# Rotating an 8192x8192 matrix: the last macro tile's outputs divided by rows in place of its loads by columns, and another rotation of the buffers at the end

## The chip, the cores and the metric

The kernel runs on one core of one Trainium2 chip. The metric is the device time of one execution in microseconds (us); lower is better. Before the change, three runs took 1270.16, 1271.46 and 1272.62 us: a median of 1271.46.

## The reference

```python
def setup_inputs():
    return {"x": np.random.randn(8192, 8192).astype(np.float32), "k": 1}

def reference(x: np.ndarray, k: int) -> np.ndarray:
    return np.rot90(x, k)
```

With k = 1 this is a turn by 90 degrees counterclockwise: out[i, j] = x[j, 8191 - i]. The kernel reads 256 MiB from HBM and writes 256 MiB; nothing is calculated.

## The kernel before

A turn is a transpose with one axis reversed. The input is cut into 16 macro tiles of 1024 rows by 4096 columns (`R` by `W`), numbered 0 to 15 (`LAST` is 15); tile m covers half the width of one band of 1024 rows. In this text (m,i) is step i of macro tile m: load (15,6) is the seventh load of the last tile, store (14,7) the last store of the one before.

**Three stages.** A load (`load`, issued by SP) brings 2 MB into a load buffer of `a_pool`: for all tiles but the last, 128 rows by 4096 columns, so that each of the 128 partitions takes one contiguous row piece of 16 KB (line 107). A reversal (`reverse`, line 111, on VectorE) copies the load buffer into `grid` with the 128 columns of each block in reversed order. `grid` holds one whole macro tile (128 KB in each partition), as 8 row blocks by 8 column chunks of 512 columns. A store (`store`) makes 2 MB of output: 32 transposes of 128x128 on TensorE (line 130) into two PSUM tiles of 128x2048, one copy of each PSUM tile into an output buffer by ScalarE (line 147), and one DMA to HBM issued by ScalarE (line 149).

**The grid is used twice over.** Even tiles store row block t in `grid[:, t]`, odd ones in `grid[:, :, t]`. Store (m,i) reads column chunk i of all eight row blocks, which is just the part of `grid` that row block i of the next tile takes. So the main loop runs, for each m under 15 and each i: issue load (m+1,i), make store (m,i), reverse load (m+1,i) into the part that the store has freed. Reversals of tile 0 come before it, the eight stores of tile 15 after it.

**A store's shape.** Store (m,i) for m under 15 covers 512 columns of the input, so 512 rows of the output, and 1024 columns of the output (the tile's 1024 input rows): a DMA of 4 x 128 pieces of 1024 numbers, 4 KB each. Output buffers are read as whole 16 KB rows by the DMA (`whole_reads` rewrites the source's access pattern so).

**The last tile.** If its stores needed all eight row blocks, as the others do, none could start before its last load. So its loads are divided by columns (lines 96 to 104): load (15,t) takes 256 rows by 2048 columns, as two pieces of 8 KB in each partition; loads 0 to 3 make the left half of the columns, 4 to 7 the right half. Stores (15,0) to (15,3) need the left half alone, (15,4) to (15,7) the right half. `chunk` translates the place in the grid (lines 83 to 84).

**Buffers.** `a_pool` and `o_pool` have two buffers of 16 KB in a partition each, taken in turn. A new load needs the load buffer of two loads before, reversed. A new store needs the output buffer of two stores before, landed in HBM. At the end, when no loads are left to be issued, stores take load buffers too (line 118): store (14,7), and stores (15,1), (15,3), (15,5), (15,7). As load (15,7) is taken ahead of store (14,7), that store gets the buffer of load (15,6), and store (15,1) that of load (15,7).

**Order.** Each engine works through its instructions in program order. SP issues loads only; ScalarE carries out the copies and issues the stores, so that a copy that waits holds up the copies and DMA issues of all later stores. Loads and stores go through one DMA queue each (q1 and q10 in the profile), on the same 16 DMA engines.

Of the kernel before, what the change touches and what calls it, by code (L numbers as in the profile page):

```python
# [2 lines left out]

# [5 lines left out]

P = 128  # L10
T = 8
R = T * P
W = 4096
C = W // T
F = 4096
FP = 2048


def whole_reads(nc):

    for fn in nc.m.functions:
        for block in fn.blocks:
            for n, ins in enumerate(block.instructions):
                if not isinstance(ins, mybir.InstDMACopy):
                    continue
                src = ins.ins[0]
                ap = [list(d) for d in src.ap]
                if len(ap) == 3 and ap[2][0] == 1 and ap[1][0] == ap[2][1]:
                    ap = [ap[0], [1, 1], [1, ap[1][1] * ap[2][1]]]
                    block.instructions[n] = copy.replace(  # L30
                        ins,
                        ins=[copy.replace(src, ap=ap)],
                        ant_dge_precooked=False,
                    )


@with_exitstack
def kernel(
    ctx: ExitStack,
    tc: tile.TileContext,  # L40
    x: bass.AP,
    k: bass.AP,
    out: bass.AP,
):

    nc = tc.nc
    assert k == 1, f"only k=1 supported, got {k}"
    nc.at_finalize(whole_reads)

    N, M = x.shape
    dt = x.dtype

    consts = ctx.enter_context(tc.tile_pool(name="consts", bufs=1))  # L60
    ident = consts.tile([P, P], dt)
    make_identity(nc, ident)
    grid = consts.tile([P, T, T, C], dt)

    a_pool = ctx.enter_context(tc.tile_pool(name="a_pool", bufs=2))
    o_pool = ctx.enter_context(tc.tile_pool(name="o_pool", bufs=2))
    psum_pool = ctx.enter_context(
        tc.tile_pool(name="psum", bufs=2, space=bass.MemoryType.PSUM)
    )

    tiles = [(r0, c0) for r0 in range(0, N, R) for c0 in range(0, M, W)]
    LAST = len(tiles) - 1
    G = F // R
    PW = FP // R
    H = T // 2

    def row_tile(m, t):

        return grid[:, t] if m % 2 == 0 else grid[:, :, t]

    def chunk(m, t, i):

        if m == LAST:
            q, t = t % 2 * H + i % H, i // H * H + t // 2
        else:
            q = i
        return grid[:, t, q] if m % 2 == 0 else grid[:, q, t]

    def load(m, t):

        r0, c0 = tiles[m]
        if m == 0 and t % 4 >= 2:
            a = o_pool.tile([P, W], dt, tag="o")
        else:
            a = a_pool.tile([P, W], dt, tag="a")
        if m == LAST:
            r0 += t % H * 2 * P
            c0 += t // H * (W // 2)
            nc.sync.dma_start(
                out=a[:].rearrange("r (t c) -> r t c", t=2),  # L100
                in_=x[r0 : r0 + 2 * P, c0 : c0 + W // 2].rearrange(
                    "(t r) c -> r t c", t=2
                ),
            )
        else:
            r0 += t * P
            nc.sync.dma_start(out=a[:], in_=x[r0 : r0 + P, c0 : c0 + W])  # L107
        return a

    def reverse(m, t, a):  # L110
        nc.vector.tensor_copy(  # L111
            out=row_tile(m, t).rearrange("r c (b m) -> r c b m", m=P),
            in_=a[:].rearrange("r (c b m) -> r c b m", c=T, m=P)[:, :, :, ::-1],
        )

    def store(m, i):
        r0, c0 = tiles[m]
        if m == LAST - 1 and i == T - 1 or m == LAST and i % 2:
            ot = a_pool.tile([P, F], dt, tag="a")
        else:  # L120
            ot = o_pool.tile([P, F], dt, tag="o")
        o = ot[:].rearrange("m (g f) -> m g f", g=G)
        ps = []
        for h in range(G // PW):
            pt = psum_pool.tile([P, FP], mybir.dt.float32, tag="ps")
            ps.append(pt[:].rearrange("m (g f) -> m g f", g=PW))

        def transposes(h, w, t):
            b = h * PW + w
            nc.tensor.transpose(  # L130
                ps[h][:, PW - 1 - w, t * P : (t + 1) * P],
                chunk(m, t, i)[:, b * P : (b + 1) * P],
                ident,
            )

        by_row = i == 0 and m < LAST
        if by_row:
            for t in range(T):
                for h in range(G // PW):
                    for w in range(PW):  # L140
                        transposes(h, w, t)
        for h in range(G // PW):
            if not by_row:
                for w in range(PW):
                    for t in range(T):
                        transposes(h, w, t)
            nc.scalar.copy(o[:, G - PW - h * PW : G - h * PW, :], ps[h])  # L147
        top = M - c0 - (i + 1) * G * P
        nc.scalar.dma_start(  # L149
            out=out[top : top + G * P, r0 : r0 + R].rearrange(  # L150
                "(g m) f -> m g f", g=G
            ),
            in_=o,
        )

    for t in range(T):
        reverse(0, t, load(0, t))
    for m in range(LAST):
        for i in range(T):
            a = load(m + 1, i)  # L160
            store(m, i)
            reverse(m + 1, i, a)
    for i in range(T):
        store(LAST, i)


# [1 line left out]
_INS = ['x', 'k']  # L168
_OUTS = [((8192, 8192), 'float32')]

_NUMBERS = {'k': 1}


# [26 lines left out]
```

## Time and profile before

| What | Value |
|---|---|
| median of three runs | 1271.46 us |
| the profiled execution's own time | 1270.38 us |
| its span | 1268.5 us |
| TensorE busy | 720.6 us (57%) |
| VectorE busy | 293.6 us (23%) |
| ScalarE busy | 466.7 us (37%) |
| HBM traffic over the span | 268.44 MB read, 268.44 MB written, 423 GB/s |
| a reversal, line 111 | 2.29 us, 128 of them |
| a copy out of PSUM, line 147 | 1.87 us, 256 of them |
| DMA issue to landing, median | load 16.7 us, store 15.9 us |

The span is cut into 40 slices of 31.7 us for the rows of digits and of GB/s. "Idle before" and the bracket at the end of a timeline's line are the time in which an engine stood still before that work, and what ended it. ACT is ScalarE, DVE VectorE, PE TensorE, SP the engine that only issues DMAs; ACTq and SPq are the instructions that issue DMAs. `ot` is an output buffer (even when it lies in `a_pool`), `a` a load buffer, `pt` a PSUM tile.

### The profile page before, as it was taken

Reading aid. Unit: us, or ns where it says so; the run is one execution under the profiler, and the core shown is the slowest. Engines: PE = TensorE matmul, PEld = TensorE weight load, DVE = VectorE, ACT = ScalarE, POOL = GpSimd, SP = SyncE. Lnnn points to the kernel's source line nnn. Section 1 sums busy time; section 2 is a strip of 40 time slices with the busy share of each in tenths; the row PEclk is TensorE's granted clock in tenths of the full one; section 3 lists DMA queues with packets and bytes.
Section 4 is the critical chain, followed back from the end, with each engine's and each line's share of the span. In section 5 each row is a group of like instructions: output and inputs, shape, how many; then the busy total and the mean of one; then the engine's idle time right before and its main releaser. Section 6 shows DMA issues by size and latency. Waiting matters only on the chain.

```text
span 1268.5 us, 9280 instructions
## 1 busy us (share of the span) xinstructions
PE 720.6 (57%) x4096; PEld 684.0 (54%) x4096; DVE 293.6 (23%) x128; ACT 466.7 (37%) x257; POOL 0.7 (0%) x6
## 2 busy tenths in 40 slices
PE   1365565565656656566566565665556655666454
PEld 1355554565545655556555554655555655655454
DVE  3322222222222222222222222222222222222120
ACT  0243333433343333333343333433343333434354
POOL 0000000000000000000000000000000000000000
PEclk9968778767686776877767778677776687778977
DMA  9999999999999999999999999999999999999989
GB/s 397 427 429 426 428 429 429 429 429 428 429 428 429 429 429 429 429 430 428 429 428 427 430 426 429 429 423 429 429 429 428 418 425 428 429 425 428 422 342 382
DMA packets 37928, 537.48 MB, mean 424 GB/s; under 512 B 4096, under 2 KB 4096, under 8 KB 4096
## 3 DMA queue, kind: packets, MB, share of 16 engines
q1 hardware_dynamic: 19456, 268.44, 49.8%
q10 hardware_dynamic: 18432, 268.44, 49.8%
q8 instruction: 32, 0.52, 0.2%
q14 instruction: 8, 0.07, 0.0%
HBM read 268.44 MB, written 268.44 MB: 423 GB/s over the span
## 4 chain that ended last, share of the span: by engine, by line
DMA 77%; ACT 18%; DVE 1%; PE 1%; issue 1%; ACTq 0%; SPq 0%; DVEq 0%
DMA out_dram<-ot 68%; ACT ot L147 18%; DMA a<-in_x_dram 9%; DVE grid L111 1%; PE pt L130 1%; ACTq L149 0%; SPq L107 0%; ACTq L147 0%; DVEq L111 0%
## 5 line engine op out<-in xcount | busy, mean ns | idle before, releaser
L130 PE MATMUL pt<-ident,grid 128*128 128x128 f32 x4096 | 720.6, 358 | 531.8 <-ACT ot L147 494.9
L130 PEld LDWEIGHTS pt<-ident,grid 128*128 128x128 f32 x4096 | 684.0, 192 | 568.2 <-ACT ot L147 528.1
L147 ACT COPY ot<-pt 128x2048 f32<-128x2048 f32 x256 | 465.5, 1870 | 748.2 <-DMA out_dram<-ot 710.7
L111 DVE COPY grid<-a 128x4096 f32<-128x4096 f32 x128 | 293.6, 2294 | 926.4 <-PE pt L130 599.4
L147 ACT ACT_TABLE_LOAD x1 | 1.3, 1283 | 39.8 <-DVE grid L111 39.8
masks.py:199 POOL TENSOR_SCALAR_AFFINE_SELECT ident<-ident 128x128 f32<-128x128 f32 x1 | 0.3, 294 | 0.1
masks.py:197 POOL MEMSET ident<- 128x128 f32 x1 | 0.2, 205 | 0.3 <-POOLq L181 0.3
L181 POOL MEMSET const-bfloat16-1.0<- 128x1 bf16 x1 | 0.1, 102 | 0.0
L181 POOL MEMSET const-uint8-127<- 128x1 uint8 x1 | 0.1, 102 | 0.0
L181 POOL MEMSET const-float32-0.0<- 128x1 f32 x1 | 0.1, 99 | 0.2 <-issue 0.2
L181 POOL MEMSET const-float32-1.0<- 128x1 f32 x1 | 0.1, 99 | 0.0
## 6 DMA issues: line engine op xcount, KB each, us to landing
a<-in_x_dram SPq DMA_DIRECT2D x128, 2048.0 KB, 16.7
out_dram<-ot ACTq DMA_DIRECT2D x128, 2048.0 KB, 15.9
```

What stands on the lines that cost most here:

```text
L111: nc.vector.tensor_copy(out=row_tile(m, t).rearrange("r c (b m) -> r c b m", m=P), in_=a[:].rearrange("r (c b m) -> r c b m", c=T, m=P)[:, ...
L130: nc.tensor.transpose(ps[h][:, PW - 1 - w, t * P : (t + 1) * P], chunk(m, t, i)[:, b * P : (b + 1) * P], ident,)
L147: nc.scalar.copy(o[:, G - PW - h * PW : G - h * PW, :], ps[h])
L181: nc = _bacc.Bacc("TRN2", target_bir_lowering=False, num_devices=1)
```

## The change

The last tile's loads become like all others: 128 rows by 4096 columns, one 16 KB piece in each partition. Its stores are divided by rows: stores (15,0) to (15,3) take the first four row blocks (512 input rows, so 512 output columns) and 1024 input columns each, so 1024 output rows; stores (15,4) to (15,7) take the other four row blocks. So such a store is a DMA of 8 x 128 pieces of 512 numbers, 2 KB each, for the same 2 MB. They need loads 0 to 3, and 4 to 7, as before. All other stores keep their shape.

The buffers are given out otherwise: store (14,7) takes an output buffer, as all stores before it; the last tile's stores take output, output, load, output, load, output, load, output buffers. By the turn of each pool store (14,7) follows store (14,5), (15,0) follows (14,6), (15,1) follows (14,7), (15,2) takes the buffer of load (15,6), (15,3) follows (15,0), (15,4) takes the buffer of load (15,7), (15,5) follows (15,1), (15,6) follows (15,2) and (15,7) follows (15,3).

The number of transposes (32 a store), the copies (two a store, 128x2048) and the number of DMAs stay.

```diff
-    def chunk(m, t, i):
+    def block(m, t, b):
 
-        if m == LAST:
-            q, t = t % 2 * H + i % H, i // H * H + t // 2
-        else:
-            q = i
-        return grid[:, t, q] if m % 2 == 0 else grid[:, q, t]
+        c, b = divmod(b, C // P)
+        at = grid[:, t, c] if m % 2 == 0 else grid[:, c, t]
+        return at[:, b * P : (b + 1) * P]
...
-        if m == LAST:
-            r0 += t % H * 2 * P
-            c0 += t // H * (W // 2)
-            nc.sync.dma_start(
-                out=a[:].rearrange("r (t c) -> r t c", t=2),
-                in_=x[r0 : r0 + 2 * P, c0 : c0 + W // 2].rearrange(
-                    "(t r) c -> r t c", t=2
-                ),
-            )
-        else:
-            r0 += t * P
-            nc.sync.dma_start(out=a[:], in_=x[r0 : r0 + P, c0 : c0 + W])
+        r0 += t * P
+        nc.sync.dma_start(out=a[:], in_=x[r0 : r0 + P, c0 : c0 + W])
...
-    def store(m, i):
+    def store(m, rows, i, pool, by_row):
+
         r0, c0 = tiles[m]
-        if m == LAST - 1 and i == T - 1 or m == LAST and i % 2:
+        r0 += rows[0] * P
+        n = len(rows) * P
+        G = F // n
+        PW = FP // n
+        if pool is a_pool:
             ot = a_pool.tile([P, F], dt, tag="a")
         else:
             ot = o_pool.tile([P, F], dt, tag="o")
...
         top = M - c0 - (i + 1) * G * P
         nc.scalar.dma_start(
-            out=out[top : top + G * P, r0 : r0 + R].rearrange(
+            out=out[top : top + G * P, r0 : r0 + n].rearrange(
                 "(g m) f -> m g f", g=G
             ),
             in_=o,
         )
 
-    for t in range(T):
+    every = list(range(T))
+    for t in every:
         reverse(0, t, load(0, t))
     for m in range(LAST):
-        for i in range(T):
+        for i in every:
             a = load(m + 1, i)
-            store(m, i)
+            store(m, every, i, o_pool, i == 0)
             reverse(m + 1, i, a)
-    for i in range(T):
-        store(LAST, i)
+    pools = [o_pool, o_pool] + [a_pool, o_pool] * 3
+    for i, pool in enumerate(pools):
+        rows = every[i // H * H :][:H]
+        store(LAST, rows, i % H, pool, False)
```

More of the change, by code (lines that the diff above doesn't have):

```diff
@@ L72 @@
     LAST = len(tiles) - 1
-    G = F // R
-    PW = FP // R
     H = T // 2
@@ L123, in store @@
         ps = []
-        for h in range(G // PW):
+        for h in range(2):
             pt = psum_pool.tile([P, FP], mybir.dt.float32, tag="ps")
@@ L128, in transposes @@
         def transposes(h, w, t):
-            b = h * PW + w
             nc.tensor.transpose(
                 ps[h][:, PW - 1 - w, t * P : (t + 1) * P],
-                chunk(m, t, i)[:, b * P : (b + 1) * P],
+                block(m, rows[t], i * G + h * PW + w),
                 ident,
             )
-        by_row = i == 0 and m < LAST
         if by_row:
-            for t in range(T):
-                for h in range(G // PW):
+            for t in range(len(rows)):
+                for h in range(2):
                     for w in range(PW):
                         transposes(h, w, t)
-        for h in range(G // PW):
+        for h in range(2):
             if not by_row:
                 for w in range(PW):
-                    for t in range(T):
+                    for t in range(len(rows)):
                         transposes(h, w, t)
@@ L154, in store @@
         )
-    for t in range(T):
+    every = list(range(T))
+    for t in every:
         reverse(0, t, load(0, t))
     for m in range(LAST):
-        for i in range(T):
+        for i in every:
             a = load(m + 1, i)
-            store(m, i)
+            store(m, every, i, o_pool, i == 0)
             reverse(m + 1, i, a)
-    for i in range(T):
-        store(LAST, i)
+    pools = [o_pool, o_pool] + [a_pool, o_pool] * 3
+    for i, pool in enumerate(pools):
+        rows = every[i // H * H :][:H]
+        store(LAST, rows, i % H, pool, False)
 _INS = ['x', 'k']
```

## The prediction

> **What bounds the kernel now.** I read the page first: the slices, then the chain of waits and the queue table.
>
> ```profile
> DMA  9999999999999999999999999999999999999989
> GB/s 397 427 429 426 428 429 429 429 429 428 429 428 429 429 429 429 429 430 428 429 428 427 430 426 429 429 423 429 429 429 428 418 425 428 429 425 428 422 342 382
> ...
> q1 hardware_dynamic: 19456, 268.44, 49.8%
> q10 hardware_dynamic: 18432, 268.44, 49.8%
> ...
> DMA 77%; ACT 18%; DVE 1%; PE 1%; issue 1%; ACTq 0%; SPq 0%; DVEq 0%
> ```
>
> The DMA engines are full from end to end, and what they move is fixed by the problem. So nothing in the engines' own work is worth time unless it lets the DMA engines go idle. The only slice that falls far below 425 to 430 GB/s, apart from the two ends, is the last but one, at 342 (slice 39, 1205 to 1237 us). I cut that end into stages with the windows view (the columns after the name of the window: its length, busy time of PE, PEld, DVE, ACT, POOL, the clock, DMA share, GB/s).
>
> ```profile
> 1125.00:1197.00 72.00, 42.98 (x275) 40.75 (x276) 12.35 (x7) 32.72 (x18) 0.00 (x0) 0.83 1.01 425
> 1197.00:1208.00 11.00, 1.62 (x15) 1.38 (x13) 2.87 (x2) 0.00 (x0) 0.00 (x0) 0.81 1.00 420
> 1208.00:1219.40 11.40, 2.32 (x11) 2.32 (x12) 5.49 (x3) 3.63 (x2) 0.00 (x0) 0.50 0.63 249
> 1219.40:1231.40 12.00, 10.81 (x87) 9.91 (x85) 0.63 (x1) 9.23 (x6) 0.00 (x0) 0.94 0.91 381
> 1231.40:1267.70 36.30, 18.67 (x160) 17.29 (x160) 0.00 (x0) 19.96 (x12) 0.00 (x0) 0.83 0.94 395
> ```
>
> Against 425 GB/s the three middle windows lose 11.0 x (1 - 420/425) = 0.1, 11.4 x (1 - 249/425) = 4.7 and 12.0 x (1 - 381/425) = 1.2 us: 6.1 us of idle DMA. The timeline of ACT says whose wait it is.
>
> ```profile
> 1191.32 3.63 ACT L147 COPY ot<-pt 128x2048 f32<-128x2048 f32 x2 [4.42 <-DMA out_dram<-ot]
> 1196.80 0.55 ACTq L149 DMA_DIRECT2D out_dram<-ot  x1
> 1215.16 3.63 ACT L147 COPY ot<-pt 128x2048 f32<-128x2048 f32 x2 [20.21 <-DVE grid L111]
> 1218.83 0.55 ACTq L149 DMA_DIRECT2D out_dram<-ot  x1
> 1220.79 3.75 ACT L147 COPY ot<-pt 128x2048 f32<-128x2048 f32 x2 [1.99 <-PE pt L130]
> 1224.57 0.55 ACTq L149 DMA_DIRECT2D out_dram<-ot  x1
> ```
>
> The copies of 1215.16 are those of store (14,7). Its output buffer is the one that load (15,6) filled, so ACT stands 20.2 us until DVE has emptied it. The DVE timeline shows that reversal starting when load 6 lands, and load 7's behind it:
>
> ```profile
> 1207.24 2.29 DVE L111 COPY grid<-a 128x4096 f32<-128x4096 f32 x1 [8.13 <-DMA a<-in_x_dram]
> 1212.79 2.29 DVE L111 COPY grid<-a 128x4096 f32<-128x4096 f32 x1 [3.25 <-DMA a<-in_x_dram]
> 1217.74 2.29 DVE L111 COPY grid<-a 128x4096 f32<-128x4096 f32 x1 [2.65 <-DMA a<-in_x_dram]
> ```
>
> Meanwhile store (14,6), issued at 1196.80, lands 11.3 us later at 1208.1, and the store queue is empty until 1218.83. One load is in flight at a time, and when load 7's data are in, nothing is.
>
> **The change, part by part.** Prices for transfers: 2 MB takes 4.9 us when the engines do nothing else (the last eight stores land 4.9 us apart: 1250.45 + 12.3 = 1262.75, 1254.76 + 12.9 = 1267.66), 9.8 us when both queues have work, and lands some 1.7 us after its last byte (store (14,7), alone: 6.6 us from issue to landing, less 4.9). With equal shares and each queue in order these rows reproduce the old end: load 7, behind load 6's data at 1211, ends at 1215.9 and lands at 1217.7, as shown.
>
> *Store (14,7) takes an output buffer.* It now waits for store (14,5), issued at 1186.93 and landed 12.8 us later, at 1199.7, in place of 1215.1. Its transposes are done by 1198.6. Copies 1199.8 to 1203.4, issue at 1203.45: 15.4 us earlier. It queues behind store (14,6), whose data end at 1206.4, and shares the engines with load 6: data until 1216.2, landing 1217.9. The sharing makes load 6 late: 1205.3 + 9.8 = 1215.1, landing 1216.9, where it landed at 1212.7. Load 7, issued at 1209.6 as before, has data from 1215.1 to 1224.9, landing 1226.6, 8.9 us late; reversed at 1229.0.
>
> *The last tile's outputs take output, output, load, output, load, output, load, output buffers.* The new waits stand in ACT's queue, and behind each stand the copies and the issues of all later stores, and PE, which waits for PSUM. Store (15,0) waits for store (14,6), 1208.1: copies to 1211.8, data 1216.2 to 1225.5. Store (15,1) waits for store (14,7), 1217.9: issued 1221.6, 3.9 us before the engines come to it; data to 1230.4. Store (15,2) waits for load 6's reversal (1219.3) and ACT: issued 1225.8, data to 1235.3. Store (15,3) waits for store (15,0), landed 1227.2: issued 1230.9, data to 1240.2. Store (15,4) needs load 7 for its rows and its buffer, 1229.0: issued about 1235.3, data to 1245.1. Then one each 4.9 us: 1250.0, 1254.9 and 1259.8 for (15,7), landing 1261.5. It landed at 1267.66: a gain of 6.2 us, close to the 6.1 us of idle DMA. All the idle is gone, since each store is issued 4 to 5 us ahead of its data.
>
> *The last tile's loads become whole rows.* A 16 KB load packet takes 611 ns (median of the packet records behind the queue table), an 8 KB one 309: two make 618. The old loads had 16 of the latter on each engine, the new 8 of the former: 56 ns a load, 8 loads, all while DMA is the bound: 0.45 us gained. SP's issue of a load goes from 0.37 us (L99) to 0.33 (L107), off the path.
>
> *The last tile's stores write rows of 2 KB in place of 4 KB*, 1,024 of them a store in place of 512. No row has a 2 KB run. Nothing can be gained by this: the same bytes in more pieces. The nearest row is that of a store packet, 16 KB read and written in four runs: 615 ns against 611 for one run, 1.3 ns for each run more. Four runs more, 8 packets to an engine and store, 8 stores: 0.35 us. If a run cost what a load's second packet does, 7 ns, it would be 1.8 us. The far end is the issue: 0.33, 0.37 and 0.55 us for 128, 256 and 512 runs; the last step goes on to 0.91 us for 1,024, and were these 0.36 us a store not covered, it would be 2.9 us. They are covered: ACT's round is 4.31 us (1233.21 to 1237.52), 4.67 then, still under DMA's 4.9. I take 0.35 and keep 0 to 2.9.
>
> The Trainium skill (DMA: Bandwidth & Descriptors, "Why small descriptors are slow (HBM only)") speaks against this part: about 3 bus cycles on top of a 32-byte beat each, per packet, and 32 bytes of metadata per descriptor. As an estimate by that page a 2 KB piece is about 3% dearer than its share of a 4 KB piece, 1.2 us over eight stores, and the time 0.85 us later than mine; for 4 KB against 16 KB the same rule would make some 2%, and the row above shows 0.7%.
>
> *Not changed:* 512 transposes in the last tile, 16 copies of 128x2048 there, DVE's 8 reversals.
>
> The sum: -6.2 - 0.45 + 0.35 = -6.3 us. The profiled execution took 1270.38 us with a span of 1268.5; the span would be 1262.2. The same on the median, 1271.46: **1265.2 us**. The profiled execution lies 1.1 under the median, which is in the runs' spread.
>
> **Rivals.** *The gap is handed on.* The output pool carries (14,7), (15,0), (15,1) and (15,3) alone, with a load buffer only for (15,2). One buffer's round is 3.65 (copies) + 1.3 (issue to data) + 4.9 + 1.7 = 11.5 us, so two buffers give a store each 5.8 us, 0.9 above 4.9. For: (15,1) now hangs on a landing. Against: 4 us of lead in the working above, and while loads share the engines, a store's data take 9.8 anyway. It decides if load 6 is reversed later than about 1226 us; four stores at 0.9 us: 1265.2 + 3.6 = 1268.8.
>
> *Slower: the 2 KB rows are not carried at full rate.* Place: the eight last stores, which run alone at the end, so nothing hides it. For: it is the one operation that no row shows. Against: 16 KB and 4 KB runs share 49.8% and 49.8% for equal bytes. At 25% more, 1.23 us a store, it costs 9.8 us: 1275.0. It decides from (6.3 + 2.5) / 8 = 1.1 us a store, 6.0 in place of 4.9; from 5.7 the change brings nothing.
>
> *It doesn't do what it says:* the idle at 1208 to 1219 stays, because something else holds store (14,7). PE's part is done at 1198.6 and store (14,5) has landed at 1199.7, so nothing is in sight. Then about 1271.
>
> **How the numbers follow.** Chances: forecast 0.66 (own range 1263.5 to 1268.1: the upper end is 2.9 us on top, the lower the spread of the times before, below), gap handed on 0.14, 2 KB rows below full rate 0.16, no effect 0.04. A measurement of this kernel tells some 0.2%, 2.5 us, from no change: faster means below 1268.9. Faster: 0.66 and 0.06 of the handed-on gap: 0.72. Within: 0.08 of it, 0.02 of 2 KB rows that cost 5 to 9 us, 0.04: 0.14. Slower: 0.14. The range, 1263.5 to 1271.5, leaves out most of the case of the 2 KB rows.
>
> **What would show it.** Right: store (14,7) is issued near 1203.5; DMA holds 425 GB/s from 1197 to 1255; loads 6 and 7 land near 1217 and 1227; ACT's wait for DVE of 20 us is gone; the last stores land 4.9 to 5.0 us apart; store packets stay within some 30 ns of 615. Wrong: landings 5.7 us apart or more (the runs), holes of a few us between 1216 and 1235 (the buffers), or an issue on ACT above 1.2 us, which would make ACT's round longer than 4.9.

## The result, and the profile after

The changed kernel took 1267.78 us (median of 17 runs, 1267.09 to 1269.78) beside 1270.62 us before (17 runs, 1269.69 to 1272.62): a ratio of 0.9977, interval 0.9970 to 0.9985. That is 2.8 us by the medians, faster as forecast, and less than half of the 6.3 us forecast. The profiled execution has a span of 1265.9 us (1268.5 before).

The page of the changed kernel, its slices, queues and chain of waits:

```profile
DMA  9999999999999999999999999999999999999989
GB/s 398 428 427 426 427 429 430 430 428 429 428 430 430 429 429 429 428 430 428 429 429 429 430 428 429 428 429 427 427 429 428 429 427 426 429 427 428 429 361 375
...
q10 hardware_dynamic: 18432, 268.44, 50.0%
q1 hardware_dynamic: 18432, 268.44, 49.7%
...
DMA 78%; ACT 19%; issue 1%; DVE 0%; ACTq 0%; PE 0%; SPq 0%
```

q1 has 1,024 packets fewer: the last tile's loads are single 16 KB packets now. But slice 39 is still low, at 361. The windows of the same stages:

```profile
1125.00:1197.00 72.00, 41.33 (x231) 39.48 (x231) 16.84 (x8) 28.65 (x16) 0.00 (x0) 0.74 1.01 428
1197.00:1208.00 11.00, 7.54 (x39) 7.30 (x39) 2.29 (x1) 4.01 (x3) 0.00 (x0) 0.66 0.95 404
1208.00:1219.40 11.40, 9.31 (x55) 9.08 (x54) 2.29 (x1) 5.50 (x3) 0.00 (x0) 0.70 0.71 299
1219.40:1231.40 12.00, 10.03 (x87) 9.24 (x86) 0.00 (x0) 9.23 (x6) 0.00 (x0) 1.00 0.97 407
```

Against 428 GB/s the last three lose 0.6, 3.4 and 0.6 us, 4.6 together; before they lost, by the same reckoning, 0.2, 4.8 and 1.3, so 6.3. The gap has become smaller, and it is another gap. ACT's timeline:

```profile
1193.74 3.63 ACT L135 COPY ot<-pt 128x2048 f32<-128x2048 f32 x2 [6.20 <-DMA out_dram<-ot]
1197.41 0.55 ACTq L137 DMA_DIRECT2D out_dram<-ot  x1
1203.56 3.63 ACT L135 COPY ot<-pt 128x2048 f32<-128x2048 f32 x2 [6.18 <-DMA out_dram<-ot]
1207.22 0.55 ACTq L137 DMA_DIRECT2D out_dram<-ot  x1
1212.20 3.63 ACT L135 COPY ot<-pt 128x2048 f32<-128x2048 f32 x2 [5.01 <-DMA out_dram<-ot]
1215.87 0.55 ACTq L137 DMA_DIRECT2D out_dram<-ot  x1
```

The three issues are stores (14,5), (14,6) and (14,7). The 20 us wait for DVE is gone, but store (14,7) is issued at 1215.9 and not at the forecast 1203.5. It waits for the landing of (14,5), as the prediction said; but (14,5) itself was issued at 1197.4, 10.5 us later than before. The loads went the other way: load (15,7) was issued at 1194.3 (1209.6 before) and landed 16.5 us later, at 1210.8 (1217.7 before). So nothing is left to be loaded from 1211 on, while stores are in flight one or two at a time. The load buffers are free again at 1204 and 1214, when VectorE has reversed loads (15,6) and (15,7), and then wait for stores (15,2) and (15,4):

```profile
1202.05 2.29 DVE L96 COPY grid<-a 128x4096 f32<-128x4096 f32 x1 [7.74 <-PE pt L119]
1212.08 2.29 DVE L96 COPY grid<-a 128x4096 f32<-128x4096 f32 x1 [7.73 <-PE pt L119]
```

What made stores later and loads earlier shows in the time from issue to landing while the last tile is being loaded. First the kernel before (loads issued from 1125 to 1215, then stores issued from 1125 to 1190), then the same two views of the changed kernel; the three numbers are least, median, most:

```profile
L99 SPq DMA_DIRECT2D a<-in_x_dram x8: 367/368/387, 1125.7 to 1209.6; - x8
DMA to landing us min/median/max: 8.1/21.5/24.7
...
L149 ACTq DMA_DIRECT2D out_dram<-ot x8: 546/546/547, 1129.5 to 1186.9; - x8
DMA to landing us min/median/max: 11.8/12.5/13.2
```

```profile
L92 SPq DMA_DIRECT2D a<-in_x_dram x8: 327/328/328, 1125.8 to 1194.3; - x8
DMA to landing us min/median/max: 16.1/16.9/17.4
...
L137 ACTq DMA_DIRECT2D out_dram<-ot x7: 546/547/547, 1128.6 to 1187.6; - x7
DMA to landing us min/median/max: 15.9/15.9/15.9
```

With 8 KB load packets a load takes 21.5 us and a store 12.5; with 16 KB packets on both queues 16.9 and 15.9. The bytes are the same. This is how the theory behind the experiments came about.

### The profile page after: what moved, and what is told of

Same layout as the page of the kernel before. It is cut to its first block, busy times and chain, and to the rows that moved or that the text cites. A ratio compares the mean times of both kernels' runs of the same rounds, so it can differ in the third digit from the quotient of the medians.

```text
span 1265.9 us, 9281 instructions
## 1 busy us (share of the span) xinstructions
PE 721.7 (57%) x4096; PEld 683.4 (54%) x4096; DVE 293.6 (23%) x128; ACT 466.6 (37%) x257; POOL 0.7 (0%) x6
## 2 busy tenths in 40 slices
DMA packets 36904, 537.48 MB, mean 425 GB/s; under 512 B 4096, under 2 KB 4096, under 8 KB 4096
## 4 chain that ended last, share of the span: by engine, by line
DMA 78%; ACT 19%; issue 1%; DVE 0%; ACTq 0%; PE 0%; SPq 0%
DMA out_dram<-ot 75%; ACT ot L135 19%; DMA a<-in_x_dram 3%; DVE grid L96 0%; PE pt L119 0%; ACTq L137 0%; SPq L92 0%; ACTq L135 0%
## 6 DMA issues: line engine op xcount, KB each, us to landing
out_dram<-ot ACTq DMA_DIRECT2D x128, 2048.0 KB, 15.9
```

## The experiments

**Theory 1, packet share:** the DMA engines serve the two queues packet by packet in turn, so the shares of bytes go as the packet sizes, 8 to 16 before and 16 to 16 after. **Theory 2:** two output buffers hand the gap on, whatever the loads. **Theory 3:** the 2 KB rows ate the gain. Every run's ratio is to the kernel before on the same chip, with its 95% interval.

**Buffers alone.** The kernel before, with the new buffers:

```diff
-        if m == LAST - 1 and i == T - 1 or m == LAST and i % 2:
+        if m == LAST and i in (2, 4, 6):
```

> Shapes as before (loads by columns in 8 KB pieces, stores with 4 KB rows), buffers given out as after. Theory 1, packet share: the DMA engines alternate between the two queues packet by packet, so 8 KB load packets get about a third of the bytes beside 16 KB store packets; loads (15,0) to (15,7) land late, stores are ahead, store (14,7) is issued near 1203.5 us and the idle of 1208 to 1219 us is gone, as the prediction's schedule has it: ratio to before 0.995 (-6 us). Theory 2, the two output buffers hand the gap on whatever the loads' shape: 0.9975, with store (14,7) at 1212 us or later. Theory 3, the shortfall of the change comes from the 2 KB rows: 0.995 too.

Measured: 1268.83 against 1271.34 us, 0.9981 (0.9972 to 0.9990). ACT's timeline of this run has the issue of store (14,7) where the prediction had it, and a new wait at store (15,4):

```profile
1202.46 0.55 ACTq L149 DMA_DIRECT2D out_dram<-ot  x1
...
1237.62 1.86 ACT L147 COPY ot<-pt 128x2048 f32<-128x2048 f32 x1 [6.46 <-PE pt L130]
1241.03 1.87 ACT L147 COPY ot<-pt 128x2048 f32<-128x2048 f32 x1 [1.55 <-PE pt L130]
1242.92 0.55 ACTq L149 DMA_DIRECT2D out_dram<-ot  x1
```

Its windows, and DVE's timeline for the two last reversals:

```profile
1197.00:1208.00 11.00, 5.61 (x50) 5.09 (x48) 4.59 (x2) 3.63 (x2) 0.00 (x0) 0.96 0.99 358
1208.00:1231.40 23.40, 14.41 (x102) 13.38 (x102) 2.29 (x1) 14.54 (x8) 0.00 (x0) 0.80 1.01 429
...
1240.00:1244.00 4.00, 3.94 (x31) 3.70 (x30) 0.00 (x0) 2.30 (x2) 0.00 (x0) 0.85 0.10 41
```

```profile
1219.20 2.29 DVE L111 COPY grid<-a 128x4096 f32<-128x4096 f32 x1 [12.47 <-DMA a<-in_x_dram]
1232.83 2.29 DVE L111 COPY grid<-a 128x4096 f32<-128x4096 f32 x1 [11.34 <-DMA a<-in_x_dram]
```

The old gap is full (429 GB/s from 1208 to 1231), but load (15,7) comes at 1232.8 in place of the 1226.6 worked out with equal shares, and its data are what store (15,4) needs: the DMA engines stand nearly idle from 1240 to 1244, which costs 3.6 us. The expected 0.995 was wrong in the same way as the prediction: it has all loads late, but takes over the prediction's schedule, in which the last load comes in time for store (15,4). The window of 1197 to 1208 loses 1.8 us more (358 GB/s) with the engines busy for 0.99 of it: some packets there took up to 1.2 us in place of 0.31 and 0.62. No run shows why. Theory 2 falls as it stood: (14,7) is early. Theory 3 is not decided here, since these holes are not those of the changed kernel.

**Shapes alone.** The changed kernel, with the buffers of before:

```diff
-            store(m, every, i, o_pool, i == 0)
+            store(m, every, i, a_pool if m == LAST - 1 and i == T - 1 else o_pool, i == 0)
...
-    pools = [o_pool, o_pool] + [a_pool, o_pool] * 3
+    pools = [o_pool, a_pool] * 4
```

> Shapes as after (whole-row loads, 2 KB rows in the last stores), buffers as before: store (14,7) takes the buffer of load (15,6). Theory 1: the loads keep half the bytes and are ahead, load 6 is reversed by 1204 us, so this buffer costs no wait; store (14,7) is issued at 1210 to 1213 us, earlier than the 1215.9 of the change: ratio 0.996 to 0.9975. Theory 2 (buffers alone decide, the loads' shape nothing): store (14,7) waits as before, near 1218 us, ratio 1.000. Theory 3 (2 KB rows cost 3.5 us): 1.002.

Measured: 1264.99 against 1271.34 us, 0.9953 (0.9941 to 0.9966): a better kernel than the changed one, and better than the 0.996 to 0.9975 expected. Its ACT timeline:

```profile
1202.71 3.63 ACT L135 COPY ot<-pt 128x2048 f32<-128x2048 f32 x2 [6.17 <-DMA out_dram<-ot]
1206.38 0.55 ACTq L137 DMA_DIRECT2D out_dram<-ot  x1
1208.34 1.87 ACT L135 COPY ot<-pt 128x2048 f32<-128x2048 f32 x1 [2.00 <-PE pt L119]
1210.83 1.87 ACT L135 COPY ot<-pt 128x2048 f32<-128x2048 f32 x1 [0.62 <-PE pt L119]
1212.73 0.55 ACTq L137 DMA_DIRECT2D out_dram<-ot  x1
1213.37 3.64 ACT L135 COPY ot<-pt 128x2048 f32<-128x2048 f32 x2 [0.67 <-ACT ot L135]
1217.04 0.55 ACTq L137 DMA_DIRECT2D out_dram<-ot  x1
```

The same statement that cost 20 us of ACT's time before, store (14,7) in load (15,6)'s buffer, costs no wait here, since the loads are ahead: its copies follow those of (14,6) as fast as PE fills PSUM. Store (15,0) follows 4.3 us behind. Theories 2 and 3 fall.

**The changed kernel with 8 KB load packets, first try.** Source and destination of each last-tile load were written as two halves of 8 KB.

> The changed kernel with one thing altered: each of the last tile's loads fetches its row piece as two packets of 8 KB. Theory 1: loads fall behind as in the kernel before (22 us to landing, reversals wait for loads), store (14,7) near 1203.5 us, no idle: ratio 0.9955, 0.0005 above the run with 4 KB rows and the same buffers. Theory 2: like the change, 0.9977 or 0.998. Theory 3: like the change or a little worse, 0.998.

Measured: 1267.98 us, 0.9977 (0.9969 to 0.9986). It says nothing of the theories: the page counts 36,904 packets, as for the change, so the halves had been joined again. It is in effect a second measurement of the change, with the same ratio.

**Whole-row loads with 4 KB output rows.** The kernel before, with the new buffers and whole-row loads:

```diff
-        if m == LAST:
+        if False:
             r0 += t % H * 2 * P
...
-        if m == LAST - 1 and i == T - 1 or m == LAST and i % 2:
+        if m == LAST and i in (2, 4, 6):
```

> The kernel before with two things altered: buffers as after, and the last tile's loads as whole rows in one 16 KB packet per partition; its stores keep 4 KB rows and their places, so the last tile's outputs hold the numbers in other places (part of the computation is left out: the order within the last tile). Theory 1: the loads are ahead as in the changed kernel, store (14,7) near 1216 us, ratio 0.9972 (the change less 0.6 us for the 2 KB rows). Theory 2: 0.9975, the same as with loads by columns. Theory 3: 0.995, since the 2 KB rows are gone.

Measured: 1267.38 us, 0.9971 (0.9960 to 0.9983), store (14,7) at 1215.65. As theory 1 has it, and the gap of the changed kernel is there without any 2 KB row. The difference to the change, 0.0006, is within the intervals.

**The store packets of tile 14 halved.** The one alteration that touches neither the division of loads and outputs nor the buffers: in `whole_reads`, the eight stores that run beside the last tile's loads get a source pattern of two pieces of 8 KB.

```diff
-                    ap = [ap[0], [1, 1], [1, ap[1][1] * ap[2][1]]]
+                    size = ap[1][1] * ap[2][1]
+                    if 14 * T <= n_store < 15 * T:
+                        ap = [ap[0], [size // 2, 2], [1, size // 2]]
+                    else:
+                        ap = [ap[0], [1, 1], [1, size]]
+                    n_store += 1
```

> The kernel before, with one thing altered: the eight stores of tile 14, which run beside the last tile's loads, read their output buffers in 8 KB packets in place of 16 KB. Shapes, places and buffers stay. Packet share: both queues then alternate with 8 KB packets and get half the bytes each, so loads (15,t) land in 16 to 17 us and not 20 to 25, load 6 is reversed by 1205 us, store (14,7) is issued at 1209 to 1213 us in place of 1218.8, and the ratio is 0.9955 (the gain of the run with the new shapes and the old buffers, 0.9953; 0.45 us lost on 8 KB packets here, 0.6 us for 2 KB rows there). Rival, the loads by columns are late for another reason (their addresses, 256 rows of 8 KB): loads still land in 20 us and more, ratio 1.000.

Measured: 1265.22 against 1271.07 us, 0.9956 (0.9943 to 0.9968), at the figure expected. The landings in the same two views, loads and stores (these issued up to 1198; the first two are tile 13's and keep 16 KB, the six others land in 14.3 to 16.9 us, median 16.0), and its windows:

```profile
L105 SPq DMA_DIRECT2D a<-in_x_dram x8: 367/368/385, 1125.5 to 1198.3; - x8
DMA to landing us min/median/max: 17.3/17.4/21.0
...
L155 ACTq DMA_DIRECT2D out_dram<-ot x8: 547/608/624, 1128.1 to 1193.5; - x8
DMA to landing us min/median/max: 11.8/16.0/16.9
```

```profile
1125.00:1197.00 72.00, 43.26 (x252) 41.36 (x253) 15.28 (x8) 28.47 (x16) 0.00 (x0) 0.74 1.01 422
1197.00:1208.00 11.00, 6.73 (x38) 6.26 (x36) 3.46 (x2) 3.63 (x2) 0.00 (x0) 0.69 1.01 425
1208.00:1219.40 11.40, 9.01 (x64) 8.49 (x64) 2.40 (x2) 8.55 (x5) 0.00 (x0) 0.85 1.01 428
```

With packets of one size on both queues, loads and stores take 17.4 and 16.0 us, though the loads are still divided by columns: it isn't their addresses. The stores have become slower and the kernel faster, because the loads are in time for store (14,7) (issued at 1211.85). No gap is left in these windows. Whether the 422 GB/s of the first window, 425 before, is a price of the smaller packets isn't shown: the run with the buffers alone, whose store packets have 16 KB, has 422 there too.

**All stores with 2 KB rows.** The kernel before, each store's DMA replaced:

```diff
-        top = M - c0 - (i + 1) * G * P
+        top = M - c0 - (i % H + 1) * T * P
+        r0 += i // H * (R // 2)
...
-            out=out[top : top + G * P, r0 : r0 + R].rearrange(
-                "(g m) f -> m g f", g=G
+            out=out[top : top + T * P, r0 : r0 + R // 2].rearrange(
+                "(g m) f -> m g f", g=T
             ),
-            in_=o,
+            in_=ot[:].rearrange("m (g f) -> m g f", g=T),
```

> The kernel before, with all 128 stores written as 8 x 128 rows of 2 KB to other places of the output (part of the computation is left out: the order of the numbers within each macro tile). It measures the price of 2 KB rows by itself. If the 11 ns that a store packet shows at the end of the changed kernel (626 in place of 615 ns) are the price everywhere: 8 packets x 11 ns = 0.09 us a store, 128 stores, 11 us, ratio 1.009. If the price vanishes beside loads: the last eight alone, ratio 1.0005. If 2 KB rows are what kept the change from its forecast (3.5 us over eight stores, 0.44 us each): 56 us, ratio 1.044.

Measured: 1281.31 against 1271.07 us, 1.0100 (1.0077 to 1.0123): 10.2 us over 128 stores, 0.08 us each, of 4.9. The queue table shows where, q10 above q1 for equal bytes:

```profile
q10 hardware_dynamic: 18432, 268.44, 50.3%
q1 hardware_dynamic: 19456, 268.44, 49.4%
```

Eight such stores cost 0.6 us; theory 3 wanted 3.5.

**The changed kernel with half-row loads.** Each last-tile load as two DMAs, so that its packets are 8 KB:

```diff
-        nc.sync.dma_start(out=a[:], in_=x[r0 : r0 + P, c0 : c0 + W])
+        n = 2 if m == LAST else 1
+        for w in range(0, W, W // n):
+            nc.sync.dma_start(
+                out=a[:, w : w + W // n],
+                in_=x[r0 : r0 + P, c0 + w : c0 + w + W // n],
+            )
```

> The changed kernel, with each load of the last tile as two DMAs of half rows, so that its packets are 8 KB; output rows of 2 KB and the buffers as in the change. Packet share: as in the run with columns and the new buffers, store (14,7) is issued at 1201 to 1205 us, load (15,7) lands at 1230 us or later, store (15,4) waits for it and the DMA idles some 3 us about 1235: ratio 0.998 to 0.9985. Rival, the column division itself made the loads late: they stay ahead as in the change, store (14,7) at 1216 us, 0.9977.

Measured: 1266.91 us, 0.9971 (0.9959 to 0.9982), half a miss. Stores land in 12.7 us (median) and load (15,7) is reversed at 1230.0, so rows in 8 KB packets are late just as columns are. But store (14,7) went out at 1211.1, not 1201 to 1205, and store (15,4) didn't have to wait: the stores were held up earlier. ACT's timeline shows copies done at 1161.5 and their DMA issued only at 1166.2:

```profile
1157.88 3.64 ACT L140 COPY ot<-pt 128x2048 f32<-128x2048 f32 x2 [4.09 <-DMA out_dram<-ot]
1166.24 0.55 ACTq L142 DMA_DIRECT2D out_dram<-ot  x1
```

By the instruction records that issue stood behind a wait for a semaphore (the counter through which a DMA reports its landing), and its DMA signals the same semaphore as an earlier load's half. With three DMAs a step in place of two, loads and stores came to share completion semaphores more often; four issues between 1166 and 1196 were held so, each 3.4 to 4.7 us after its copies were done. From 1185 to 1197 the DMA moved only 382 GB/s, though its engines were busy for 0.99 of the time: why it moved less is not shown. The effect of the semaphores was not tried by itself.

**One half-row load.** The shapes-alone kernel, with only load (15,7) cut in two (`n = 2 if m == LAST and t == T - 1`).

> The changed shapes with the buffers of before (ratio 0.9953 in its own run), and load (15,7) alone as two DMAs of half rows, in 8 KB packets. It lets stores (14,5) and (14,6) run faster beside the last load. Packet share: store (14,6)'s copies start up to 2 us earlier, up to 1 us of the idle left at 1206 to 1212 goes, ratio 0.9945 to 0.9953. Rival: nothing left to gain there, or load 7 late: 0.9953 to 0.996.

Measured: 1265.51 us, 0.9959 (0.9946 to 0.9971). No gain can be told, and the figure lies with the rival, not in the 0.9945 to 0.9953 of packet share. Store (14,6)'s copies waited 5.6 us for a landing where they waited 6.2 with the shapes alone, so 0.6 of the hoped-for 2 us came, and idle time remains: 393 GB/s from 1206 to 1212, 410 with the shapes alone.

## Why the prediction was right, and where its size was off

The measured time lies in the range and on the side forecast. The gain is 2.8 us where the sum said 6.3; point by point:

**Right: the bound and the place.** The DMA engines' idle time at the end decides. What ended the old gap, store (14,7)'s wait for load (15,6), is gone. In the changed kernel it went by the new buffer; the run with the shapes alone shows that the whole-row loads end it without that.

**The step that failed** is the sentence that with equal shares and each queue in order the rows reproduce the old end, and what was built on it: store (14,7) "now waits for store (14,5), issued at 1186.93 and landed 12.8 us later, at 1199.7". That time was taken from a kernel whose loads had 8 KB packets. The same change turns them into 16 KB ones; loads then get an equal share, stores take 15.9 us and not 12.5, and (14,5) is issued 10.5 us later and lands at 1212.1. The price of the load packets was counted as 0.45 us of engine time and nothing else; that they also divide the engines between the queues was left out, though the figures to see it were in the trace before (12.8 us for a store beside 21.4 for load 5). The term of -6.2 us measured -1.7 between 1197 and 1231 (6.3 us of idle before, 4.6 after).

**A price that was misread.** "Lands some 1.7 us after its last byte" is the whole of what store (14,7)'s 6.6 us have beyond 4.9. By the packet records its first packet starts 1.2 us after the issue and its last one ends 0.4 us before the landing. The sum is hardly touched, since its ends of data and its landings differ by the same 1.7 throughout. But the rival's round of 11.5 us adds 1.3 us from issue to data to that 1.7, and so counts the start twice: 10.2 us, 5.1 a store and not 5.8. The range's lower end, 1263.5, is 1.7 us under the forecast, where the spread of the times before is 1.3 below; nothing hung on it.

**The two parts of the change work against each other.** Buffers alone: 0.9981. Shapes alone: 0.9953. Both: 0.9977. With late loads the old buffers are wrong (store (14,7) waits for a load), with loads in time the new ones (store (14,7) waits for a store until 1212 while load (15,6)'s buffer stands empty from 1204). The rival in which the gap is handed on through the output pool came nearest in kind, but not by its condition: load 6's buffer was free at 1204, not after 1226.

**The 2 KB rows** were taken at 0.35 us with bounds of 0 and 2.9, and measure 0.6 (0.08 a store). The last stores land 5.0 us apart (from 1226.28 + 8.8 = 1235.1 to 1252.24 + 12.8 = 1265.0, six steps), 4.9 before. The Trainium skill's rule (DMA: Bandwidth & Descriptors, "Why small descriptors are slow (HBM only)") gave an estimate of 1.2 us: right in sign, twice too much. The upper end of the bound, a longer issue on ACT, was empty: 0.547 us for 1,024 rows, as for 512.

**The load packets** were put at 0.45 us: the first window's 425 GB/s became 428, 72 us x 3/428 = 0.5 us. The runs agree in the sign but spread as widely: 425, 422 and 422 GB/s in the three with 8 KB loads by columns (before, buffers alone, store packets halved), 428 and 429 with whole rows (after, shapes alone).

These terms make 1.7 + 0.5 - 0.6 = 1.6 of the 2.8 us between the medians, and of the 2.6 us between the two profiled spans. Of the latter a further 1 us was already there at 1125 us, ahead of everything that the change touches (418 GB/s in one slice of the old profile, with no counterpart in the new). Profiles of the same DMAs differ by as much: at 1125 us the run whose halves were joined again had 0.8 MB more left to move than the changed kernel, 1.9 us at 428 GB/s. So this 1 us need not be the change's; where the rest of the 2.8 us between the medians lies stays open.

## What to carry to other kernels

When a change alters the packet size of one of two busy DMA queues, it can alter their shares, as here, and then no landing time of the old trace holds for the new kernel: work the schedule out again with the new shares, up to the last transfer. At the end of a DMA-bound kernel take as an output's buffer whichever comes free first, and ask that again after every change of shape.

## What the runs showed of the hardware

**The packet sizes of two busy queues tilt their shares.** 8 KB load beside 16 KB store packets: 21.5 us to landing for a load, 12.5 for a store; 16 beside 16: 16.9 and 15.9; 8 beside 8: 17.4 and 16.0. By the packet records the loads moved 169 GB/s and the stores 255 from 1135 to 1195 before, 212 and 217 after, and 208 and 212 from 1150 to 1200 with 8 beside 8: two to three, not one to two, with unlike packets, and nearly equal parts with like ones. The Trainium skill (DMA: Bandwidth & Descriptors, "Queues, rings and completion order") says that each engine takes turns between queues, a whole packet at a time; these rows agree in the direction, though none of them shows the turns one by one, with a packet being here one contiguous piece of the DMA's source in one partition, as the profile counts them (the store's source rewritten in halves gave 1,024 packets more).

**A DMA can wait for a stranger.** In the kernel before, store (14,6)'s copies were done by 1195.0, yet its DMA was issued at 1196.80, as load (15,4) landed. The view of line 149 between 1125 and 1260 counts the waits of this kind:

```profile
L149 ACTq EVENT_SEMAPHORE  x2: 17/17/17, 1196.7 to 1222.7; - x2
```

By the instruction records the load and the store signal the same semaphore, and the store's issue is held until the load has landed. Of the two waits there only the first held an issue, by 1.8 us: the second's load had landed at 1207.2, before ACT came to it. With half-row loads there are 11, of which four held one.
